# Seven block products instead of eight in the gate and up projections of one FFN

## The chip, the cores and the metric

The kernel runs on one core of a Trainium2 chip. The metric is the time of one execution on the device, in microseconds (us). The times of the kernel before were 2115.74, 2116.9 and 2116.8 us, median 2116.8.

## The reference

Two transformer blocks over 512 tokens of width 1024, in float32. The change touches one piece of the first block, its second feed-forward layer:

```
u = modulate(rmsnorm(h, norm3_g), shift, scale)
h = h + 0.5 * gate * ((silu(u @ w_g) * (u @ w_u)) @ w_down)
```

`w_g` and `w_u` are the two halves of `ffn2_w_gu`, each 1024 x 2816; `w_down` is 2816 x 1024. The feature dimension 2816 is 22 tiles of 128.

## The kernel before, in words

Activations lie with features on the 128 partitions and the 512 tokens along the row, so `h` is eight tiles of 128x512. Every float32 operand of a large product is cut into a rounded part `hi` (type float32r) and the rest `lo`, and a product is three matmuls: hi x hi, hi x lo and lo x hi. For weights `split_w` does this: ScalarE rounds a 128x1024 piece (L131), VectorE subtracts (L132). Split weights live in two rings of four buffers (`whi`, `wlo`), raw weights in a ring of two (`raw`), loaded by SP's queue.

`proj` (L155 to L164) forms one 128x512 result in a PSUM bank: for each of the eight k tiles three matmuls of 512 columns. `ffn_first` runs the layer. For each feature tile f it loads the gate and the up columns, splits them, calls `proj` twice, takes Silu on ScalarE (L482), multiplies on VectorE (L484) and splits the result (L485, L486) into `m_hi`, `m_lo`. After 8, 16 and 22 tiles a down projection adds that part to `h` (L497): eight output tiles j, with 8, 8 and 6 k tiles; in the last part the tiles j = 6 and 7 go in two halves of 256 columns. In the second layer (`halved=True`) the first feature tile is also worked in two halves of tokens, because `u` becomes available half by half: `Modulated` gathers the row statistics while `h` is being finished, and `modulate` makes `hi` and `lo` of `u` from them (L304, L307, L308).

The order of instructions on each engine is made by a planner that walks the program in order and takes, at each step of its own timeline, the first instruction that is ready; waits are semaphores between the engines. POOL, whose queue issues the DMAs that the hardware generators can't do, has no work in this stage.

Of the kernel before, what the change touches and what calls it, by code (L numbers as in the profile page):

```python
# [25 lines left out]
def kernel(  # L26
# [7 lines left out]
    nc = tc.nc  # L34
# [6 lines left out]
    sp = ctx.enter_context(tc.tile_pool(name="sp", bufs=2))  # L41
# [40 lines left out]
    with tc.tile_pool(name="stage", bufs=1) as stage:  # L82
# [16 lines left out]
        def raw_tile():  # L99
            return wp.tile([P, 8 * 256], F32, tag="raw", name="w_raw")  # L100
# [23 lines left out]
        def split_w(src, hi=None, lo=None):  # L124
            if hi is None:
                shape = [P, src.shape[1], src.shape[2]]
                hi, lo = (
                    wp.tile([P, 8 * P], F32R, tag=tag, name=tag, bufs=4)[
                        :, 0:shape[1] * shape[2]].rearrange("p (k n) -> p k n", n=shape[2])
                    for tag in ("whi", "wlo"))  # L130
            nc.scalar.activation(out=hi, in_=src, func=AF.Copy)  # L131
            nc.vector.tensor_tensor(out=lo, in0=src, in1=hi.bitcast(F32), op=ALU.subtract)  # L132
            return hi, lo

        def by_feature(raw, kt=KT):
            v = raw[:, 0:kt * 256].rearrange("p (k n) -> p k n", n=256)
            return [split_w(v[:, :, r * P:(r + 1) * P]) for r in range(2)]
# [17 lines left out]
        def proj(acc, w, u, k0=0, cols=slice(0, S)):  # L155
            whi, wlo = w
            n = len(u)
            for k in range(n):
                uhi, ulo = u[k]
                a = whi[:, k0 + k, :]  # L160
                b = wlo[:, k0 + k, :]
                nc.tensor.matmul(acc, lhsT=a, rhs=uhi[:, cols], start=k == 0, stop=False)  # L162
                nc.tensor.matmul(acc, lhsT=a, rhs=ulo[:, cols], start=False, stop=False)  # L163
                nc.tensor.matmul(acc, lhsT=b, rhs=uhi[:, cols], start=False, stop=k == n - 1)  # L164
# [13 lines left out]
        def split_act(src, pool, tag, bufs=None):  # L178
            kw = {} if bufs is None else {"bufs": bufs}
            hi = pool.tile([P, S], F32R, tag=tag + "h", name=tag + "_hi", **kw)  # L180
            lo = pool.tile([P, S], F32R, tag=tag + "l", name=tag + "_lo", **kw)
            nc.scalar.activation(out=hi, in_=src, func=AF.Copy)
            nc.vector.tensor_tensor(out=lo, in0=src, in1=hi.bitcast(F32), op=ALU.subtract)
            return hi, lo
# [51 lines left out]
        def shift(sub, j):  # L236
            f = (sub * 3) * KT + j
            return modc[:, f:f + 1]

        def gmod(sub, j):  # L240
            return gmod_t[:, sub, j:j + 1]

        def gate(sub, j):
            return gate_t[:, sub, j:j + 1]


        h = [hp.tile([P, S], F32, name=f"h{j}") for j in range(KT)]
# [23 lines left out]
        class Stat:  # L271
            def __init__(self):
                self.acc = sp.tile([P, S], F32, tag="acc", name="acc", bufs=2)

            def add(self, j, cols=ALL, scale=1.0):
                if j == 0:
                    nc.scalar.activation(out=self.acc[:, cols], in_=h[j][:, cols], func=AF.Square,
                                         scale=scale)
                    return
                sq = sp.tile([P, S], F32, tag="wk", name="sq")  # L280
                nc.scalar.activation(out=sq[:, cols], in_=h[j][:, cols], func=AF.Square,
                                     scale=scale)
                nc.vector.tensor_add(out=self.acc[:, cols], in0=self.acc[:, cols],
                                     in1=sq[:, cols])
# [11 lines left out]
        def new_u():  # L296
            return [tuple(up.tile([P, S], F32R, tag=tag, name=tag) for tag in ("uh", "ul"))
                    for _ in range(KT)]
# [19 lines left out]
        class Modulated:  # L318
# [13 lines left out]
            def operand(self):  # L332
                u = new_u()
                for pb, cols in self.pieces:
                    modulate(self.sub, u, pb, cols)
                return u

        def down_tiles(src, kt, by_halves=True):

            pieces = {}  # L340
            steps = [(j, ALL) for j in range(KT)]
            if by_halves:
                steps = steps[:6] + [(j, cols) for cols in HALVES for j in range(6, KT)]
            for j, cols in steps:
                q = j // 2
                if q not in pieces:
                    pieces[q] = by_feature(load_w(src[:, 256 * q:256 * (q + 1)], kt, 256), kt)
                yield j, cols, pieces[q][j % 2]
# [110 lines left out]
    parts = ((0, 8), (8, 16), (16, 22))  # L459


    def ffn_first(u, w_gu, w_down, sub, on_final, nxt=None, side=None, early=(), halved=False):
        with tc.tile_pool(name=f"ffn{sub}", bufs=2) as fp:
            for pi, (f0, f1) in enumerate(parts):
                ms = []
                for f in range(f0, f1):
                    if f < len(early):
                        raw = early[f]
                    else:
                        raw = load_pair(w_gu[:, f * P:(f + 1) * P],  # L470
                                        w_gu[:, FF + f * P:FF + (f + 1) * P], KT, P)
                    wg, wu = by_feature(raw)
                    hi = fp.tile([P, S], F32R, tag="mh", name="m_hi", bufs=14)
                    lo = fp.tile([P, S], F32R, tag="ml", name="m_lo", bufs=14)
                    for cols in HALVES if halved and f == 0 else (ALL,):
                        n = cols.stop - cols.start
                        pg = mm_bank()[:, 0:n]
                        proj(pg, wg, u, cols=cols)
                        pu = mm_bank()[:, 0:n]
                        proj(pu, wu, u, cols=cols)  # L480
                        sg = fp.tile([P, S], F32, tag="sg", name="sg")[:, 0:n]
                        nc.scalar.activation(out=sg, in_=pg, func=AF.Silu)  # L482
                        m = fp.tile([P, S], F32, tag="m", name="m")[:, 0:n]
                        nc.vector.tensor_mul(out=m, in0=sg, in1=pu)  # L484
                        nc.scalar.activation(out=hi[:, cols], in_=m, func=AF.Copy)  # L485
                        nc.vector.tensor_tensor(out=lo[:, cols], in0=m,  # L486
                                                in1=hi[:, cols].bitcast(F32), op=ALU.subtract)
                    ms.append((hi, lo))
                    if side is not None:
                        side(f, fp)  # L490
                kt = f1 - f0
                last = pi == len(parts) - 1
                for j, cols, w in down_tiles(w_down[f0 * P:f1 * P], kt, last):
                    pd = mm_bank()[:, 0:cols.stop - cols.start]
                    with behind(nxt, j, cols):
                        proj(pd, w, ms, cols=cols)
                    nc.vector.scalar_tensor_tensor(out=h[j][:, cols], in0=pd,  # L497
                                                   scalar=gate(sub, j), in1=h[j][:, cols],
                                                   op0=ALU.mult, op1=ALU.add)
                    if last:  # L500
                        on_final(j, cols)
# [17 lines left out]
    with ExitStack() as mx:  # L519
# [140 lines left out]
        with tc.tile_pool(name="mrg", bufs=2) as gp:  # L660
# [28 lines left out]
            for j, cols, w in down_tiles(w_out[0], KT):  # L689
# [3 lines left out]
                nc.vector.scalar_tensor_tensor(out=h[j][:, cols], in0=pd, scalar=gate(1, j),  # L693
                                               in1=h[j][:, cols], op0=ALU.mult, op1=ALU.add)
                nxt.add(j, cols)
    u = nxt.operand()


    wi = w_in_2[0]
# [21 lines left out]
            u2[j] = tuple(up.tile([P, S], F32R, tag=tag, name=tag) for tag in ("uh", "ul"))  # L721
        scaled(j, gcomb, u2[j], cols)

    ffn_first(u, ffn2_w_gu[0], ffn2_w_down[0], 2, end_of_first, halved=True)
    u = u2

    def bcast_sb(inv, pool):
# [517 lines left out]
```

## Time and profile before

| what | value |
|---|---|
| median of 3 runs | 2116.8 us |
| the profiled execution | 2115.97 us |
| its span | 2114.3 us |
| granted TensorE clock, mean | 0.996 of 2.4 GHz |
| TensorE, VectorE, ScalarE, POOL busy | 99%, 55%, 39%, 4% |

The span is measured inside the execution; 1.7 us lie around it. A matmul's busy time overlaps with the next one's, so the cost of a matmul is read from the distance of two starts. The changed layer stands at about 781 to 1147 us of the span.

### The profile page before, as it was taken

Reading aid. Unit: us, or ns where it says so; the run is one execution under the profiler, and the core shown is the slowest. Engines: PE = TensorE matmul, PEld = TensorE weight load, DVE = VectorE, ACT = ScalarE, POOL = GpSimd, SP = SyncE. Lnnn points to the kernel's source line nnn. Section 1 sums busy time; section 2 is a strip of 40 time slices with the busy share of each in tenths; the row PEclk is TensorE's granted clock in tenths of the full one; section 3 lists DMA queues with packets and bytes.
Section 4 is the critical chain, followed back from the end, with each engine's and each line's share of the span. In section 5 each row is a group of like instructions: output and inputs, shape, how many; then the busy total and the mean of one; then the engine's idle time right before and its main releaser. Section 6 shows DMA issues by size and latency. Waiting matters only on the chain.

```text
span 2114.3 us, 24896 instructions
## 1 busy us (share of the span) xinstructions
PE 2086.4 (99%) x9814; PEld 1698.0 (80%) x9814; DVE 1163.6 (55%) x1988; ACT 824.4 (39%) x1284; POOL 94.1 (4%) x156
## 2 busy tenths in 40 slices
PE   7999999999999999999999999999999999999998
PEld 5778888888878888888888876767888888888888
DVE  3775645466653454333336486746454566474675
ACT  4322222357653333222225354645233344242454
POOL 1000000000000000000000011112200000000000
PEclk9999999999999999999999999999999999999999
DMA  9776654331122333333322332213323333333332
GB/s 347 217 226 179 179 179 119 101 99 61 60 81 81 101 99 82 98 100 100 100 85 95 97 94 80 80 50 100 120 80 100 100 85 96 100 100 100 90 106 94
DMA packets 302216, 235.72 MB, mean 111 GB/s; under 512 B 6821, under 2 KB 289130, under 8 KB 301844
## 3 DMA queue, kind: packets, MB, share of 16 engines
q1 hardware_dynamic: 298752, 223.96, 35.2%
q0 software_dynamic: 2656, 9.09, 1.3%
q8 instruction: 77, 1.26, 0.3%
q10 hardware_dynamic: 692, 1.09, 0.1%
q14 instruction: 39, 0.32, 0.0%
HBM read 229.89 MB, written 4.23 MB: 111 GB/s over the span
## 4 chain that ended last, share of the span: by engine, by line
PE 97%; ACT 1%; DVE 1%; DMA 1%; issue 0%; POOL 0%; POOLq 0%; SPq 0%; ACTq 0%; DVEq 0%
PE mm_ps L162 27%; PE mm_ps L163 27%; PE mm_ps L164 27%; PE mm_ps L174 2%; PE mm_ps L175 2%; PE mm_ps L176 2%; PE po_ps L929 2%; PE z_ps L604 1%; PE z_ps L922 1%; PE z_ps L883 1%; PE po_ps L615 1%; PE z_ps L885 1%; DMA wa<-in_w_ada_dram 0%; PE z_ps L207 0%; PE z_ps L1044 0%
## 5 line engine op out<-in xcount | busy, mean ns | idle before, releaser
L131 ACT ACTIVATE whi<-w_raw 128x1024 fp32r<-128x1024 f32 (+1 forms) x350 | 365.0, 1045 | 892.2 <-PE mm_ps L163 694.1
L162 PE MATMUL mm_ps<-uh,whi 128*128 128x512 f32 (+1 forms) x1680 | 653.3, 391 | 3.8 <-ACT uh L307 3.3
L163 PE MATMUL mm_ps<-ul,whi 128*128 128x512 f32 (+1 forms) x1680 | 653.9, 390 | 0.0
L164 PE MATMUL mm_ps<-uh,wlo 128*128 128x512 f32 (+1 forms) x1680 | 653.2, 389 | 0.0
L132 DVE TENSOR_TENSOR wlo<-w_raw,whi 128x1024 fp32r<-128x1024 f32 (+1 forms) x350 | 426.6, 1221 | 233.6 <-ACT whi L131 227.9
L162 PEld LDWEIGHTS mm_ps<-uh,whi 128*128 128x128 f32 x1680 | 316.1, 189 | 71.4 <-ACT uh L307 4.7
L164 PEld LDWEIGHTS mm_ps<-uh,wlo 128*128 128x128 f32 x1680 | 316.8, 189 | 64.9 <-issue 1.6
L163 PEld LDWEIGHTS mm_ps<-ul,whi 128*128 128x128 f32 x1680 | 316.8, 189 | 63.5 <-issue 0.8
L164 PE MATMUL mm_ps<-m_hi,wlo 128*128 128x512 f32 (+1 forms) x564 | 212.1, 376 | 0.0
L162 PE MATMUL mm_ps<-m_hi,whi 128*128 128x512 f32 (+1 forms) x564 | 211.7, 377 | 0.0
L163 PE MATMUL mm_ps<-m_lo,whi 128*128 128x512 f32 (+1 forms) x564 | 211.6, 375 | 0.0
L163 PEld LDWEIGHTS mm_ps<-m_lo,whi 128*128 128x128 f32 x564 | 106.1, 188 | 20.1 <-issue 0.4
L164 PEld LDWEIGHTS mm_ps<-m_hi,wlo 128*128 128x128 f32 x564 | 106.1, 188 | 19.9
L162 PEld LDWEIGHTS mm_ps<-m_hi,whi 128*128 128x128 f32 x564 | 106.0, 188 | 19.8 <-issue 0.8
L174 PE MATMUL mm_ps<-whi,uh 128*128 128x512 f32 (+1 forms) x288 | 99.9, 350 | 3.6 <-ACT whi L131 1.6
L175 PE MATMUL mm_ps<-wlo,uh 128*128 128x512 f32 (+1 forms) x288 | 98.7, 344 | 0.8 <-DVE wlo L132 0.8
L176 PE MATMUL mm_ps<-whi,ul 128*128 128x512 f32 (+1 forms) x288 | 97.4, 343 | 0.0
L497 DVE SCALAR_TENSOR_TENSOR h<-mm_ps,gate,h 128x512 f32<-128x512 f32 (+1 forms) x52 | 36.9, 709 | 100.5 <-PE mm_ps L164 100.3
L484 DVE TENSOR_TENSOR m<-sg,mm_ps 128x512 f32<-128x512 f32 (+1 forms) x45 | 30.4, 675 | 107.8 <-PE mm_ps L164 107.2
L200 DVE SCALAR_TENSOR_TENSOR ada_acc<-ada_w,csil,ada_acc 128x256 f32<-128x256 f32 x196 | 87.4, 482 | 1.9
L1118 DVE SCALAR_TENSOR_TENSOR y<-xp,cols_c,y 128x512 f32<-128x512 f32 x88 | 65.7, 749 | 2.3 <-ACT y L1114 0.7
L174 PEld LDWEIGHTS mm_ps<-whi,uh 128*128 128x128 f32 x288 | 54.4, 189 | 11.3 <-ACT uh L307 2.0
(314 smaller groups left out, 2304.0 us busy)
## 6 DMA issues: line engine op xcount, KB each, us to landing
w_raw<-in_ffn_w_gu_dram SPq DMA_DIRECT2D x88, 512.0 KB, 5.2
ada_w<-in_w_ada_dram SPq DMA_DIRECT2D x28, 1024.0 KB, 5.2
w_raw<-in_w_up_dram SPq DMA_DIRECT2D x44, 512.0 KB, 5.2
w_raw<-in_w_in_dram SPq DMA_DIRECT2D x20, 1024.0 KB, 5.2
w_raw<-in_ffn_w_down_dram SPq DMA_DIRECT2D x16, 1024.0 KB, 5.1
w_raw<-in_w_mix_in_dram SPq DMA_DIRECT2D x24, 512.0 KB, 5.3
wa<-in_w_ada_dram SPq DMA_DIRECT2D x8, 1024.0 KB, 11.2
w_raw<-in_w_mix_in_dram SPq DMA_DIRECT2D x8, 1024.0 KB, 5.0
```

The lines of the kernel that those rows point to most:

```text
L131: nc.scalar.activation(out=hi, in_=src, func=AF.Copy)
L132: nc.vector.tensor_tensor(out=lo, in0=src, in1=hi.bitcast(F32), op=ALU.subtract)
L162: nc.tensor.matmul(acc, lhsT=a, rhs=uhi[:, cols], start=k == 0, stop=False)
L163: nc.tensor.matmul(acc, lhsT=a, rhs=ulo[:, cols], start=False, stop=False)
L164: nc.tensor.matmul(acc, lhsT=b, rhs=uhi[:, cols], start=False, stop=k == n - 1)
L174: nc.tensor.matmul(acc, lhsT=a, rhs=wh, start=k == 0, stop=False)
L175: nc.tensor.matmul(acc, lhsT=a, rhs=wl, start=False, stop=False)
L176: nc.tensor.matmul(acc, lhsT=b, rhs=wh, start=False, stop=k == kt - 1)
L200: nc.vector.scalar_tensor_tensor(out=acc[:, q, :], in0=v[:, k, :], scalar=csil[:, k:k + 1], in1=acc[:, q, :], op0=ALU.mult, op1=ALU.add)
L497: nc.vector.scalar_tensor_tensor(out=h[j][:, cols], in0=pd, scalar=gate(sub, j), in1=h[j][:, cols], op0=ALU.mult, op1=ALU.add)
L929: nc.tensor.matmul(po[64 * hd:64 * hd + 64, b * P:S], lhsT=vts[head // 4][:, b, c0:c0 + 64], rhs=pT, start=b == 0, stop=b == NB - 1, skip_ ...
L1118: nc.vector.scalar_tensor_tensor(out=y, in0=xp[:, k:k + S], scalar=cols_c[:, 44 * k + col:44 * k + col + 1], in1=y, op0=ALU.mult, op1=ALU.add)
```

## The change

In `ffn_seven` twenty of the 22 feature tiles are worked in pairs. The product of a pair's weights with `u` is taken as a 2 x 2 block product: upper and lower block row are the 256 gate and the 256 up columns, the inner dimension is cut into its two halves of 512, the tokens into two halves of 256. Strassen's scheme (in Winograd's form) forms it with seven block products instead of eight. Each block product (`times`) is two row tiles x four k tiles x three matmuls of 256 columns.

- **Sums of `u`** (`operand`): made once, for each of four k, four VectorE operations of 128x256, one rounding of 128x1024 on ScalarE and one subtraction on VectorE. They need `u` unsplit, so `modulate_full` writes it with one more ScalarE instruction per tile and half. The sums stand in the ring `ra` of four buffers, before the blocks `w11` and `w21` of the weights use it.
- **Sums of weights**: four DMAs per pair, issued by POOL, SBUF to SBUF with `accum_op=add`, 128x1024 floats each. Splits in order: `w11`, `w12`, then after adds `w11`, `w21`, `w11`, `w11`, and `w22`: seven of 128x1024 per pair instead of four.
- **Recombining**: three ScalarE copies out of PSUM and five VectorE sums or differences of 128x512 per pair.
- The first two tiles stay as they were, the first in halves. The down projections come after 6, 12, 18 and 22 tiles, each one pair of gate and up products later than its data.

```diff
+            p1 = split_w(w11)
+            add(w11, w21)
+            ca = z_bank()
+            self.times(ca, p1, self.plain(0, H1), True)
+            v1 = copy(ca)
+            p2 = split_w(w12)
+            self.times(ca, p2, self.plain(HK, H1), False)
+            upper(ca, 0)
+            q7 = split_w(w11)
+            add(w21, w22)
+            add(w11, w22)
+            cd = z_bank()
+            self.times(cd, q7, self.diff(2), True)
+            v7 = copy(cd)
+            q5 = split_w(w21)
+            cc = z_bank()
+            self.times(cc, q5, self.diff(0), True)
+            v5 = copy(cc)
+            q6 = split_w(w11)
+            add(w11, w12)
+            cb = z_bank()
+            self.times(cb, q6, self.diff(1), True)
+            nc.vector.tensor_add(out=v1, in0=v1, in1=cb)
+            nc.vector.tensor_add(out=v5, in0=v5, in1=v1)
+            nc.vector.tensor_sub(out=v7, in0=v7, in1=v5)
+            q3 = split_w(w11)
+            self.times(cc, q3, self.plain(HK, H2), False)
+            nc.vector.tensor_add(out=v5, in0=cc, in1=v1)
+            upper(v5, 1)
+            lower(v7, 1)
+            q4 = split_w(w22)
+            self.times(cd, q4, self.diff(3), False)
+            nc.vector.tensor_sub(out=v1, in0=cd, in1=v1)
+            lower(v1, 0)
...
+        def operand(self, u, full):
+            self.u = u
+            for k in range(HK):
+                t = self.pool.tile([P, 4, 256], F32, tag="ra", name="usum", bufs=4)
...
+                nc.vector.tensor_sub(out=t[:, 0], in0=b11, in1=b12)
+                nc.vector.tensor_sub(out=t[:, 2], in0=b12, in1=b22)
+                nc.vector.tensor_sub(out=t[:, 1], in0=t[:, 2], in1=b11)
+                nc.vector.tensor_add(out=t[:, 3], in0=t[:, 1], in1=b21)
...
+            def add(to, of):
+                nc.gpsimd.dma_start(out=to, in_=of, accum_op=ALU.add)
...
+            nc.scalar.activation(out=hi, in_=t, func=AF.Identity, bias=shift(sub, j))
+            nc.scalar.activation(out=full[j][:, cols], in_=t, func=AF.Identity,
+                                 bias=shift(sub, j))
+            nc.vector.tensor_tensor(out=lo, in0=full[j][:, cols], in1=hi.bitcast(F32),
+                                    op=ALU.subtract)
...
+            bounds = ((0, 6), (6, 12), (12, 18), (18, 22))
+            pairs = [eight_pair(0)]
+            seven.operand(u, full)
+            for f0, f1 in bounds:
+                last = f1 == NF
+                for f in range(f0 + 2, min(f1 + 2, NF), 2):
+                    pairs.append(seven_pair(f))
...
-    ffn_first(u, ffn2_w_gu[0], ffn2_w_down[0], 2, end_of_first, halved=True)
+    ffn_seven(nxt, ffn2_w_gu[0], ffn2_w_down[0], 2, end_of_first)
```

## Rows read from the trace of the kernel before

**Rows 1.** The page's busy table and the chain that ended last.
```profile
PE 2086.4 (99%) x9814; PEld 1698.0 (80%) x9814; DVE 1163.6 (55%) x1988; ACT 824.4 (39%) x1284; POOL 94.1 (4%) x156
...
PE 97%; ACT 1%; DVE 1%; DMA 1%; issue 0%; POOL 0%; POOLq 0%; SPq 0%; ACTq 0%; DVEq 0%
```

**Rows 2.** Windows: stretch, busy of each engine, granted clock, DMA share, GB/s.
```profile
800.00:930.00 130.00, 129.86 (x578) 107.41 (x578) 47.10 (x51) 35.86 (x44) 0.00 (x0) 1.00 0.34 97
```

**Rows 3.** Waits, 790 to 1160 us: who waited for whom, total, times, longest.
```profile
ACT whi L131 <- PE mm_ps L163: 180.8, 48, 6.1
DVE wlo L132 <- ACT whi L131: 82.2, 44, 4.9
```

**Rows 4.** Timeline of ScalarE: start, duration, instruction; Silus of whole tiles.
```profile
815.43 0.58 ACT L482 ACTIVATE sg<-mm_ps 128x512 f32<-128x512 f32 x1
...
869.83 0.58 ACT L482 ACTIVATE sg<-mm_ps 128x512 f32<-128x512 f32 x1
```

**Rows 5.** Timeline of TensorE, last down projection, matmuls of 256 columns.
```profile
1143.39 0.28 PE L164 MATMUL mm_ps<-m_hi,wlo 128*128 128x256 f32 x1
...
1146.63 0.28 PE L164 MATMUL mm_ps<-m_hi,wlo 128*128 128x256 f32 x1
```

**Rows 6.** Lines by form, 790 to 1160 and 781 to 810 us: busy, mean ns.
```profile
L131 ACT ACTIVATE whi<-w_raw 128x1024 fp32r<-128x1024 f32 x60 | 63.6, 1061 | 218.9 <-PE mm_ps L163 158.3 <-issue 60.6
L132 DVE TENSOR_TENSOR wlo<-w_raw,whi 128x1024 fp32r<-128x1024 f32 x60 | 73.5, 1227 | 76.6 <-ACT whi L131 75.0
L497 DVE SCALAR_TENSOR_TENSOR h<-mm_ps,gate,h 128x512 f32<-128x512 f32 x22 | 16.5, 751 | 57.4 <-PE mm_ps L164 57.3
L484 DVE TENSOR_TENSOR m<-sg,mm_ps 128x512 f32<-128x512 f32 x21 | 14.4, 688 | 70.4 <-PE mm_ps L164 70.4
L486 DVE TENSOR_TENSOR m_lo<-m,m_hi 128x512 fp32r<-128x512 f32 x21 | 14.4, 685 | 0.0
L485 ACT ACTIVATE m_hi<-m 128x512 fp32r<-128x512 f32 x21 | 13.3, 631 | 0.2
L482 ACT ACTIVATE sg<-mm_ps 128x512 f32<-128x512 f32 x21 | 12.2, 582 | 0.0
L283 DVE TENSOR_TENSOR acc<-acc,sq 128x256 f32<-128x256 f32 x8 | 3.1, 418 | 0.0
...
L307 ACT ACTIVATE uh<-ut,modc 128x256 fp32r<-128x256 f32 x16 | 7.6, 504 | 6.6 <-DVE ut L304 6.6
```

**Rows 7.** DMA issues: transfer, queue, times, KB each, median us to landing.
```profile
w_raw<-in_ffn_w_gu_dram SPq DMA_DIRECT2D x88, 512.0 KB, 5.2
...
cb<-cum_d POOLq DMA_DIRECT2D x16, 256.0 KB, 3.5
...
w_raw<-in_w_ple_gate_dram SPq DMA_DIRECT2D x4, 1024.0 KB, 8.4
...
pl<-ple_d POOLq DMA_DIRECT2D x1, 2048.0 KB, 8.3
...
wsr<-in_gmlp_w_s_dram POOLq DMA_DIRECT2D x1, 512.0 KB, 4.3
...
gfb<-in_norm_final_g_dram POOLq DMA_DIRECT2D x1, 512.0 KB, 10.6
```

**Rows 8.** Lines of POOL: the issue of a DMA.
```profile
L871 POOL DMA_DIRECT2D cb<-cum_d x16 | 9.0, 563 | 122.3 <-DVE low L893 54.1 <-issue 39.6 <-DVE off L889 23.4
```

**Rows 9.** Windows at the stage's start, columns as in rows 2.
```profile
781.00:790.00 9.00, 7.43 (x46) 7.16 (x47) 8.27 (x20) 4.46 (x11) 0.70 (x1) 0.81 0.44 117
790.00:800.00 10.00, 9.67 (x65) 8.76 (x64) 7.53 (x18) 5.64 (x11) 0.00 (x0) 1.00 0.01 2
```

**Rows 10.** Timeline of VectorE at the stage's start; in brackets the idle time before.
```profile
797.76 0.49 DVE L308 SCALAR_TENSOR_TENSOR ul<-ut,modc,uh 128x256 fp32r<-128x256 f32 x1 [0.18 <-ACT uh L307]
803.13 1.22 DVE L132 TENSOR_TENSOR wlo<-w_raw,whi 128x1024 fp32r<-128x1024 f32 x1 [4.89 <-ACT whi L131]
```

More of the change, by code (lines that the diff above doesn't have):

```diff
@@ L459, with ffn_first @@
     parts = ((0, 8), (8, 16), (16, 22))
-    def ffn_first(u, w_gu, w_down, sub, on_final, nxt=None, side=None, early=(), halved=False):
+    def ffn_first(u, w_gu, w_down, sub, on_final, nxt=None, side=None, early=()):
         with tc.tile_pool(name=f"ffn{sub}", bufs=2) as fp:
@@ L472, in ffn_first @@
                     wg, wu = by_feature(raw)
[L473 to L488, printed above, removed]
+                    pg = mm_bank()
+                    proj(pg, wg, u)
+                    pu = mm_bank()
+                    proj(pu, wu, u)
+                    sg = fp.tile([P, S], F32, tag="sg", name="sg")
+                    nc.scalar.activation(out=sg, in_=pg, func=AF.Silu)
+                    m = fp.tile([P, S], F32, tag="m", name="m")
+                    nc.vector.tensor_mul(out=m, in0=sg, in1=pu)
+                    ms.append(split_act(m, fp, "m", 14))
                     if side is not None:
@@ new lines, in modulate_full @@
+    def modulate_full(sub, u, full, pb, cols):
+        for j in range(KT):
+            hi, lo = (t[:, cols] for t in u[j])
+            t = sp.tile([P, S], F32, tag="wk", name="ut")[:, cols]
+            nc.vector.scalar_tensor_tensor(out=t, in0=h[j][:, cols], scalar=gmod(sub, j),
+                                           in1=pb[:, 0:cols.stop - cols.start],
+                                           op0=ALU.mult, op1=ALU.mult)
+            nc.scalar.activation(out=hi, in_=t, func=AF.Identity, bias=shift(sub, j))
[3 more added lines that the diff above has]
+                                    op=ALU.subtract)
@@ new lines, in ffn_seven, with split_m, m_pair, eight_pair @@
+    def ffn_seven(nxt, w_gu, w_down, sub, on_final):
+        with tc.tile_pool(name=f"ffn{sub}", bufs=4) as fp:
+            u = new_u()
+            full = []
+            for _ in range(HK):
+                t = fp.tile([P, 2, S], F32, tag="mh", name="u_full")
+                full += [t[:, 0], t[:, 1]]
+            for pb, cols in nxt.pieces:
+                modulate_full(sub, u, full, pb, cols)
+            seven = Seven(fp)
+            def split_m(m, hi, lo):
+                nc.scalar.activation(out=hi, in_=m, func=AF.Copy)
+                nc.vector.tensor_tensor(out=lo, in0=m, in1=hi.bitcast(F32), op=ALU.subtract)
+            def m_pair():
+                return tuple(fp.tile([P, 2, S], F32R, tag=tag, name=name)
+                             for tag, name in (("mh", "m_hi"), ("ml", "m_lo")))
+            def eight_pair(f0):
+                pair = m_pair()
+                for r in range(2):
+                    f = f0 + r
+                    wg, wu = by_feature(load_pair(w_gu[:, f * P:(f + 1) * P],
+                                                  w_gu[:, FF + f * P:FF + (f + 1) * P], KT, P))
+                    for cols in (ALL,) if r else HALVES:
+                        n = cols.stop - cols.start
+                        pg = mm_bank()[:, 0:n]
+                        proj(pg, wg, u, cols=cols)
+                        pu = mm_bank()[:, 0:n]
+                        proj(pu, wu, u, cols=cols)
+                        sg = seven.ev()[:, 0:n]
+                        nc.scalar.activation(out=sg, in_=pg, func=AF.Silu)
+                        nc.vector.tensor_mul(out=sg, in0=sg, in1=pu)
+                        split_m(sg, *(t[:, r, cols] for t in pair))
+                return pair
+            def seven_pair(f0):
+                pair = m_pair()
+                cols = slice(f0 * P, (f0 + 2) * P)
+                weights = seven.load(w_gu[:, cols], w_gu[:, FF + f0 * P:FF + (f0 + 2) * P])
+                sg = {}
+                def upper(src, half):
+                    sg[half] = src if half else seven.ev()
+                    nc.scalar.activation(out=sg[half], in_=src, func=AF.Silu)
+                def lower(src, half):
+                    nc.vector.tensor_mul(out=src, in0=src, in1=sg[half])
+                    split_m(src.rearrange("p (r s) -> p r s", r=2),
+                            *(t[:, :, HALVES[half]] for t in pair))
+                seven.run(weights, upper, lower)
+                return pair
+            bounds = ((0, 6), (6, 12), (12, 18), (18, 22))
[5 more added lines that the diff above has]
+                    pairs.append(seven_pair(f))
+                kt = f1 - f0
+                ms = [tuple(t[:, r, :] for t in pair) for pair in pairs[:kt // 2]
+                      for r in range(2)]
+                del pairs[:kt // 2]
+                for j, cols, w in down_tiles(w_down[f0 * P:f1 * P], kt, last):
+                    pd = mm_bank()[:, 0:cols.stop - cols.start]
+                    proj(pd, w, ms, cols=cols)
@@ L695 @@
                 nxt.add(j, cols)
-    u = nxt.operand()
     wi = w_in_2[0]
```

63 lines of the change are left out of this document (added).

## The prediction

> **What bounds the kernel now.** I read the page's busy table and its chain of waits first, then the stage, then the spacing of matmuls, then the engines beside them. TensorE is busy 99% of the span and holds 97% of the chain that ended last [rows 1]: time goes only where matmuls go, or where TensorE is made to wait. The changed stage runs from about 781 us (first modulated operand) to 1147 us (last down projection). Inside it TensorE is busy 129.86 of 130 us while VectorE has 47.10 and ScalarE 35.86, at a granted clock of 1.00, the upper level, 2.4 GHz [rows 2]. The split of a weight tile (ScalarE L131, VectorE L132) waits longest for a matmul that frees its buffer [rows 3]: weights are ahead of TensorE. So the stage is a dense stream of matmuls with spare room on VectorE, ScalarE and the DMA engines (share 0.34).
>
> **Matmuls removed.** Successive Silus of whole tiles stand 10.88 us apart (815.43 to 869.83 us, five steps) [rows 4]; a tile has 48 matmuls of 512 columns, so one costs 226.7 ns. The matmuls of 256 columns in the last down projection start at 1143.39 and, 27 later, 1146.63 us [rows 5]: 120.0 ns. Half the columns cost 0.53 of the time, about 13 ns fixed each. A pair of tiles was 96 x 0.2267 = 21.76 us. Seven products of 2 rows x 4 k x 3 matmuls are 168 x 0.120 = 20.16 us, not 7/8 of 21.76 (19.04). Gain 1.60 us a pair, 16.0 us for ten pairs. The last down part shrinks from 6 to 4 k tiles, so 72 matmuls in halves become 48: 24 fewer, each 120.0 - 113.4 ns too dear, 0.2 us. Other down matmuls are only regrouped. TensorE gain: 16.2 us.
>
> The Trainium skill (TensorE: Matmul & The Clock Gate, Back-to-back issue gap) has a gap of columns / 2.4 GHz plus 2.5 ns, 215.8 and 109.2 ns here; by it a pair would save 20.72 - 18.35 = 2.37 us, the sum 23.7 us. The trace has 226.7 and 120.0 ns, so I keep 16.0.
>
> **VectorE and ScalarE.** Per pair now: seven splits of 128x1024, 1.061 us on ScalarE and 1.227 us on VectorE each, instead of four; five recombining operations of 128x512 at 0.688 us, two products at 0.688, two subtractions at 0.685; on ScalarE three copies at about 0.6, two Silus at 0.582, two roundings at 0.631 [rows 6]. VectorE 8.6 + 3.4 + 1.4 + 1.4 = 14.8 us, ScalarE 7.4 + 1.8 + 1.2 + 1.3 = 11.7 us, in 20.16 us of matmuls. Neither is the bound by itself. Eight more updates of h, 0.751 us each, lie beside the down matmuls. Without that cover the added VectorE work, 7 us a pair, would be 70 us.
>
> **The adding DMAs.** Four a pair, 512 KB each, on POOL's queue, whose issue takes 0.56 us [rows 8] and delays nothing (POOL has no other work here). They are in a chain: split p1, add, split q7, add, split q6, add, split q3. No row shows a DMA that adds, nor one from SBUF to SBUF. On that queue 256 KB land in 3.5 us, 512 KB in 4.3, 2048 KB in 8.3 [rows 7]. An add reads source and destination and writes one. Lower bound 3.5 us, upper 8.3. Nearest are 4.3 (bytes counted once) and 4.3 + 512/1536 x 4.0 = 5.6 (twice); I take L = 5.0.
>
> Does L fit? A product lasts 24 x 0.120 = 2.88 us. Four buffers for split weights let a split start when the product four earlier ends, three products before its own. With p1 starting at 0, q7's split may start at -2.88, q3 is due at 14.4. Between lie three splits (1.061 + 1.227 = 2.29 each) and two adds: q3 is ready at -2.88 + 6.87 + 2L, late by 2L - 10.4 us. At L = 5.0 that is 0.4 us of slack; it runs out at 5.2. One evacuation of 0.69 us ahead of the split on VectorE uses up the 0.4 and leaves 0.3; six pairs do not follow a down projection: 1.8 us. The three that do have 1.2 us more, as down products (18 x 0.2267 = 4.08 us) free buffers earlier relative to them. Bounds: 0 at 3.5; at 8.3, 6 x 6.2 + 3 x 5.0 = 52 us.
>
> **The start.** Modulation is a ping-pong of ut, uh, ul. The copy `full` adds 16 x 0.504 = 8.1 us to ScalarE [rows 6], which between 781 and 800 us is busy 4.46 + 5.64 of 19 [rows 9]: it fits, but nearly fills it, and ul now waits behind it. Taken: 1.5 us (0 if it falls into the idle pieces, 8.1 if all of it lengthens the ping-pong). Then the operand sums: 16 x 0.418 + 4 x 1.227 = 11.6 us of VectorE, which today idles 4.89 us from 798.25 to 803.13 us [rows 10]. The sums use the four "ra" buffers that w11 and w21 of the first pair need. Step by step: sums 0 and 1 from 799.5 us, lo 0 done at 804.1, lo 1 with a weight split between about 807; w11 lands 5.2 us later [rows 7] at 809.3, w21 at 812.2. p1 is split at 811.6. TensorE would be done with the first two tiles at 815.43 - 5.44 = 810.0 (24 matmuls before the Silu of the third): waits 1.6. p2 ends at 817.4; add 1 lands at 817.2, q7 is split at 819.5: 2.1. Add 2 lands at 822.2, q5 is split at 824.5 against 822.4: 2.1. q6 is ready at 826.8, in time (827.4). Add 4 lands at 831.8, q3 is split at 834.1 against 830.3: 3.8. Into this last wait the next pair's p1 and p2 can be ordered, which need no new sum; I count it as filled. Cost 1.5 + 1.6 + 2.1 + 2.1 = 7.3 us; 11.1 with nothing filled, 0 if sums and loads were hidden, 21 at the upper L. The clock may add to it: over 781 to 790 us, where TensorE waits now, the grant was 0.81 [rows 9]; once more of that would be 9 x 0.19 = 1.7 us, which I leave to the range.
>
> **The end.** The last pair is consumed at once. After its last matmul come a subtraction, a product and a rounding (0.69 + 0.69 + 0.63 us and hand-overs, 2.4 together); the two k tiles of the pair before give 6 x 0.2267 = 1.4 us of cover: 1.0 us (0 if another j's first matmuls are put there, 1.7 with the lo part). Today seven k tiles cover it.
>
> **Sum.** -16.2 + 7.3 + 1.8 + 1.0 = -6.1 us against the profiled execution, 2115.97 us (span 2114.3, 1.7 around it): 2109.9. The median shown, 2116.8, lies 0.8 above it, so on its scale 2110.7.
>
> **Rivals.** Differences within 0.2%, 4.2 us, cannot be told from none, so faster means below 2112.6, slower above 2121.0.
>
> *The adds are too slow (slower).* Place: q3 of each pair, and q7 of the first. With nothing filled in, the sum passes zero at L of about 5.4 and +4.2 us at about 5.7. At L = 6: 6 x 1.6 + 3 x 0.4 = 10.8 us late, start 1.5 + 1.6 + 3.1 + 3.1 + 4.8 = 14.1, end 1.0, less 16.2: +9.7, 2126.5. At L = 7: 28.8 + 17.1 + 1.0 - 16.2 = +30.7, 2147.5. For it: an add moves more than a plain copy of its size, and adds travel beside weight loads. When a 2048 KB and a 512 KB transfer ran on POOL's queue near the end, the 512 KB took 10.6 us and the weight loads beside them 8.4 instead of 5.2 [rows 7]. Against: the stage's DMA share is 0.34, and TensorE's order can put p1 and p2 of the next pair, 5.8 us, ahead of a late q3. Chance 0.28.
>
> The Trainium skill (DMA: Bandwidth & Descriptors, Issuing engines are not separate DMA queues) says that DMAs from all issuing engines run on the same 16 engines and interleave. The trace's 8.4 and 10.6 us agree.
>
> *The gain is spent at the start.* Nothing fills the wait for q3 (11.1 us) and VectorE's order costs each of ten pairs one 0.3 us: -16.2 + 11.1 + 3.0 + 1.0 = -1.1, 2115.7. For it: a 73% busy in-order VectorE. Against: it has whole stretches under the down matmuls. Chance 0.22.
>
> *The start is hidden.* Sums go into VectorE's 4.89 us gap and the loads land in time, only q7 waits 2.1: 2103.7. Against: buffers tie the loads to the sums. Chance 0.10.
>
> Forecast 0.40, own range 2107 to 2114.
>
> **Numbers.** Faster: 0.36 of the forecast and the hidden start, 0.46. Same: 0.04 of it, 0.16 of the spent gain, 0.01 of the slow adds, 0.21. Slower: 0.27 and 0.06, 0.33. The range leaves out half of the hidden start and the worst of the slow adds (L above about 6.6): 2103 to 2140.
>
> **What would show it.** Right: matmuls of 256 columns 120 ns apart and 20.2 us between pairs in the middle of the stage; adds landing in about 5 us; TensorE idle 5 to 9 us around 800 to 835 us and hardly after. Wrong: adds over 5.6 us with TensorE waiting on VectorE L132 in each pair; 256-column matmuls dearer than 120 ns; or a granted clock below 1 after the waits.

## The result and the profile after

The changed kernel takes 2170.3 us (median of 4 runs, 2168.69 to 2173.78), the kernel before 2116.27 us beside it: ratio 1.0258, 95% interval 1.024 to 1.0275. It is slower by 54 us, where the forecast was 6 us faster and the range ended at 2140. The profiled execution took 2169.28 us, its span is 2167.5 us, 53.2 us more than before. All times are medians; one run each of vector_adds and last_by_vector below, at a mean granted clock of 0.65, took about 2950 us and is left out of theirs.

The page of the changed kernel, busy table and chain of waits (they answer to [rows 1]):

```profile
PE 2099.1 (97%) x10522; PEld 1737.5 (80%) x10522; DVE 1242.4 (57%) x2104; ACT 882.7 (41%) x1372; POOL 127.7 (6%) x196
...
PE 47%; ACT 1%; issue 1%; DVE 1%; DMA 0%; POOL 0%; POOLq 0%; ACTq 0%; DVEq 0%
```

TensorE is no longer busy all the time, and its share of the chain that ended last falls from 97% to 47%: the shares listed make up half of the span, and the rest has no line of its own there, so the page only says that matmuls are no longer all of the path. VectorE and ScalarE hardly moved, so neither has become the bound by its load. The stage tells more. Windows of the changed kernel, columns as in [rows 2]:

```profile
800.00:850.00 50.00, 41.27 (x269) 38.01 (x268) 27.81 (x37) 21.17 (x28) 6.23 (x7) 0.91 0.62 150
850.00:900.00 50.00, 42.15 (x302) 40.45 (x302) 23.88 (x28) 19.26 (x25) 4.35 (x5) 0.92 0.61 150
900.00:950.00 50.00, 50.00 (x299) 44.74 (x298) 26.29 (x31) 16.63 (x21) 4.36 (x5) 1.00 0.53 137
950.00:1000.00 50.00, 41.60 (x299) 39.98 (x298) 23.58 (x28) 20.56 (x27) 6.09 (x7) 0.90 0.61 138
1000.00:1050.00 50.00, 49.77 (x274) 44.08 (x274) 25.09 (x30) 13.62 (x17) 3.48 (x4) 0.97 0.57 151
1050.00:1100.00 50.00, 43.16 (x322) 41.72 (x321) 26.93 (x31) 21.14 (x28) 6.10 (x7) 0.93 0.62 145
1100.00:1150.00 50.00, 47.05 (x247) 40.67 (x247) 25.24 (x30) 15.71 (x20) 3.48 (x4) 0.97 0.43 112
```

TensorE idles 8.7 + 7.9 + 0 + 8.4 + 0.2 + 6.8 + 3.0 = 35 us, and the granted clock falls short of 1.00 by 0.09 + 0.08 + 0 + 0.10 + 0.03 + 0.07 + 0.03, times 50 us: by that estimate 20 us more. The fullest stretches hold a down projection. How one leads to the other, windows of 2 us in the second pair:

```profile
844.00:846.00 2.00, 0.00 (x0) 0.00 (x0) 0.00 (x0) 1.00 (x2) 0.82 (x1) 1.00 0.01 2
...
848.00:850.00 2.00, 2.00 (x12) 2.00 (x11) 0.00 (x0) 0.17 (x1) 0.47 (x1) 0.50 0.93 172
...
852.00:854.00 2.00, 2.00 (x19) 2.00 (x18) 0.51 (x2) 1.12 (x2) 0.00 (x0) 1.00 0.28 74
```

TensorE stands still at 844 to 846 us; at 848 to 850 us the grant is 0.50, the level of 1.2 GHz, and 12 matmuls fall into the window, against 19 at 2.4 GHz (852 to 854 us). So a part of the waits is paid a second time. Who waits for whom, 781 to 1210 us ([rows 3] of before; `z_ps` is the PSUM bank of a block product, L536 its first matmul of three; `uth` and `utl` below are the parts of the sums of `u`):

```profile
ACT whi L131 <- DMA w_sum<-w_raw: 69.5, 28, 5.7
...
ACT whi L131 <- DMA w_sum<-w_sum: 30.4, 7, 8.3
PE z_ps L536 <- ACT whi L131: 29.1, 19, 3.0
```

Before, the splits waited for TensorE; now ScalarE's split waits for the adds (99.9 us), and TensorE for the split (29.1 us in 19 stops). The adds themselves, DMA issues of the same stretch ([rows 7]):

```profile
w_sum<-w_raw POOLq DMA_DIRECT2D x30, 512.0 KB, 4.6
...
w_sum<-w_sum POOLq DMA_DIRECT2D x10, 512.0 KB, 6.7
```

The median is 4.6 us for the second to fourth add of a pair, 6.7 us for the first. One period, from the second pair's first add to the third pair's. POOL's issues of adds 1 to 4 and of the next add 1, start and, in brackets, the idle time before:

```profile
835.29 0.87 POOL L578 DMA_DIRECT2D w_sum<-w_sum  x1 [8.62 <-DVE wlo L132]
845.17 0.87 POOL L578 DMA_DIRECT2D w_sum<-w_raw  x1 [9.01 <-DMA w_sum<-w_sum]
847.60 0.87 POOL L578 DMA_DIRECT2D w_sum<-w_raw  x1 [1.56 <-DVE wlo L132]
855.15 0.87 POOL L578 DMA_DIRECT2D w_sum<-w_raw  x1 [6.68 <-DVE wlo L132]
865.74 0.87 POOL L578 DMA_DIRECT2D w_sum<-w_sum  x1 [9.71 <-DVE wlo L132]
```

and ScalarE's splits in the same stretch (and of its other instructions the copies of p1's product, 845.96, and of q5's, 856.76):

```profile
845.00 1.06 ACT L131 ACTIVATE whi<-w_sum 128x1024 fp32r<-128x1024 f32 x1 [2.22 <-DMA w_sum<-w_sum]
845.96 0.58 ACT L582 ACTIVATE ev<-z_ps 128x512 f32<-128x512 f32 x1
...
849.83 1.06 ACT L131 ACTIVATE whi<-w_sum 128x1024 fp32r<-128x1024 f32 x1 [3.29 <-DMA w_sum<-w_raw]
...
852.54 1.06 ACT L131 ACTIVATE whi<-w_sum 128x1024 fp32r<-128x1024 f32 x1 [0.69 <-DMA w_sum<-w_raw]
...
856.76 0.60 ACT L582 ACTIVATE ev<-z_ps 128x512 f32<-128x512 f32 x1 [2.22 <-PE z_ps L543]
860.25 1.06 ACT L131 ACTIVATE whi<-w_sum 128x1024 fp32r<-128x1024 f32 x1 [2.90 <-DMA w_sum<-w_raw]
861.22 1.04 ACT L131 ACTIVATE whi<-w_raw 128x1024 fp32r<-128x1024 f32 x1
862.16 1.04 ACT L131 ACTIVATE whi<-w_sum 128x1024 fp32r<-128x1024 f32 x1
```

Read together they are one chain. From the issue of add 1 to the start of q7's split, which needs it, pass 9.71 us; to q5's split, which needs add 2, 4.83 more; to q6's, which needs add 3, 2.71; to the issue of add 4 2.61; to q3's split, which needs it, 5.10. Behind q3's split stand q4's, the third pair's p1 (862.16) and p2, and the next add 1 goes out 5.49 after q3's split began. Sum 30.45 us, where TensorE needs 20.16. This period is the longest: the six of the stage that hold no down projection last 24.5 to 30.5 us. The third pair's p1 needs no sum at all. Its weights' load was issued at 832.75 us, and the buffer that it takes, the fourth before it, is that of q5, whose product is done when it is copied out at 856.76. It is split at 862.16, because it stands behind q3 and q4 on ScalarE, which works in order.

Not only splits stand behind a waiting split. TensorE's stop in this period is

```profile
846.10 0.39 PE L536 MATMUL z_ps<-uth,whi 128*128 128x256 f32 x1 [2.81 <-ACT whi L131]
```

on q7's first matmul. p2's product, 2.88 us of work, could have filled it, for p2 had been split since 836.1 us. But on TensorE it stands behind q7's first two matmuls, and it needs the bank of p1's product copied out, which ScalarE does at 845.96, behind q7's split. What another order there would give was not tried.

### The profile page after: what moved, and what is told of

Same layout as the page of the kernel before. It is cut to its first block, busy times and chain, and to the rows that moved or that the text cites. A ratio compares the mean times of both kernels' runs of the same rounds, so it can differ in the third digit from the quotient of the medians.

```text
span 2167.5 us, 26690 instructions
## 1 busy us (share of the span) xinstructions
PE 2099.1 (97%) x10522; PEld 1737.5 (80%) x10522; DVE 1242.4 (57%) x2104; ACT 882.7 (41%) x1372; POOL 127.7 (6%) x196
## 4 chain that ended last, share of the span: by engine, by line
PE 47%; ACT 1%; issue 1%; DVE 1%; DMA 0%; POOL 0%; POOLq 0%; ACTq 0%; DVEq 0%
PE mm_ps L162 12%; PE mm_ps L164 12%; PE mm_ps L163 12%; PE mm_ps L174 2%; PE mm_ps L175 2%; PE mm_ps L176 2%; PE po_ps L1133 2%; PE z_ps L1126 1%; PE z_ps L1087 1%; PE z_ps L1089 1%; PE z_ps L543 0%; PE z_ps L541 0%; PE z_ps L536 0%; PE z_ps L1248 0%; DMA w_sum<-w_raw 0%
## 5 line engine op out<-in xcount | busy, mean ns | idle before, releaser
L131 ACT ACTIVATE whi<-w_raw 128x1024 fp32r<-128x1024 f32 (+2 forms) x338 | 344.4, 1023 | 704.7 <-PE mm_ps L163 550.4
L162 PE MATMUL mm_ps<-uh,whi 128*128 128x512 f32 (+1 forms) x1360 | 529.4, 391 | 5.1 <-ACT uh L307 2.0
L163 PE MATMUL mm_ps<-ul,whi 128*128 128x512 f32 x1360 | 529.5, 390 | 0.0
L164 PE MATMUL mm_ps<-uh,wlo 128*128 128x512 f32 x1360 | 528.4, 389 | 0.0
L132 DVE TENSOR_TENSOR wlo<-w_raw,whi 128x1024 fp32r<-128x1024 f32 (+2 forms) x338 | 402.3, 1193 | 149.7 <-ACT whi L131 145.6
L162 PEld LDWEIGHTS mm_ps<-uh,whi 128*128 128x128 f32 x1360 | 255.8, 189 | 60.7 <-ACT uh L307 3.9
L164 PEld LDWEIGHTS mm_ps<-uh,wlo 128*128 128x128 f32 x1360 | 256.0, 188 | 52.1 <-issue 1.6
L162 PE MATMUL mm_ps<-m_hi,whi 128*128 128x512 f32 (+1 forms) x560 | 211.6, 381 | 0.9 <-ACT whi L131 0.5
L162 PEld LDWEIGHTS mm_ps<-m_hi,whi 128*128 128x128 f32 x560 | 105.4, 188 | 21.1 <-ACT whi L131 0.9
L132 DVE TENSOR_TENSOR wlo<-w_sum,whi 128x1024 fp32r<-128x1024 f32 x50 | 61.2, 1225 | 103.8 <-ACT whi L131 103.0
L536 PE MATMUL z_ps<-uth,whi 128*128 128x256 f32 x320 | 94.6, 296 | 18.7 <-ACT whi L131 18.6
L174 PE MATMUL mm_ps<-whi,uh 128*128 128x512 f32 (+1 forms) x288 | 100.7, 353 | 5.9 <-ACT zv L1190 2.9
L131 ACT ACTIVATE whi<-w_sum 128x1024 fp32r<-128x1024 f32 x50 | 52.9, 1058 | 126.4 <-DMA w_sum<-w_raw 69.5
L543 PE MATMUL z_ps<-uth,wlo 128*128 128x256 f32 x320 | 93.7, 293 | 3.6 <-DVE wlo L132 3.6
L541 PE MATMUL z_ps<-utl,whi 128*128 128x256 f32 x320 | 92.8, 290 | 0.0
```

The costliest lines, as they stand in the source:

```text
L174: nc.tensor.matmul(acc, lhsT=a, rhs=wh, start=k == 0, stop=False)
L536: i = nc.tensor.matmul(a, lhsT=whi[:, k, rows], rhs=uhi, start=start and first is None, stop=False, skip_group_check=True)
L541: nc.tensor.matmul(a, lhsT=whi[:, k, rows], rhs=ulo, start=False, stop=False, skip_group_check=True)
L543: nc.tensor.matmul(a, lhsT=wlo[:, k, rows], rhs=uhi, start=False, stop=last, skip_group_check=True)
```

## The experiments

Theory 1: the order of the splits ties the adds of one pair and the first add of the next into one serial chain, which is longer than TensorE's work. Rivals: the adds' traffic slows TensorE, the loads or the buffers (theory 2); or the scheme itself (more splits, recombining, regrouped down projections) costs the time (theory 3). All were timed in three rounds beside the kernel before; the intervals are 95%.

**no_adds**: everything but the adds, so the sums of weights are not formed and the result is not the layer's.

```diff
-                nc.gpsimd.dma_start(out=to, in_=of, accum_op=ALU.add)
+                pass
```

> Leaves out the four adding DMAs of each pair, so the block products are of the blocks as loaded (their sums are not formed); everything else stays. Theory 1 (the chain: a pair lasts as long as add, split, add, split, add, split in a row, because ScalarE splits the next pair's p1 only behind q3, which waits for the last add): the chain is gone, the pair is bound by its 168 matmuls of 120 ns, 20.2 us; the stage keeps -16.2 us and pays about 5 us at its start and end: 2104 to 2112. Theory 2 (transfers: the adding DMAs are late because they share the engines with weight loads, whatever the order): the same 2104 to 2112. Theory 3 (no gain to be had: short matmuls, VectorE and ScalarE work eat it): above 2125 with TensorE still waiting for splits.

Measured 2105.57 us, ratio 0.9952 (0.9937 to 0.9967); the span is 2103.5 us. Its first window of 50 us:

```profile
800.00:850.00 50.00, 50.00 (x388) 48.44 (x387) 36.41 (x47) 28.23 (x37) 0.00 (x0) 1.00 0.39 122
```

TensorE is full at 1.00, and so it is in the five windows up to 1100 us. So the adds cost 65 us, and the scheme without them is 10 us faster than the kernel before. Splits and recombining are hidden. Theories 1 and 2 expect this alike; theory 3 is out.

**vector_adds**: the same sums, made by VectorE.

```diff
-                nc.gpsimd.dma_start(out=to, in_=of, accum_op=ALU.add)
+                nc.vector.tensor_add(out=to, in0=to, in1=of)
```

> The same sums by VectorE (four tensor_add of 128x1024, about 1.23 us each) instead of DMAs; the result is complete. Theory 1: each add step shrinks from 5 to 9 us to about 1.5, the chain of a pair to 3 x (1.5 + 2.3) + 5 = 16 us, under 20.2; VectorE has 14.8 + 4.9 = 19.7 us a pair and is nearly the bound: 2106 to 2118. Theory 2: no added transfers: 2106 to 2118 as well. Theory 3: VectorE becomes the bound, above 2130.

Measured 2108.38 us, ratio 0.9962 (0.995 to 0.9975): faster than both kernels. Lines by form of this kernel, busy and mean ns:

```profile
L578 DVE TENSOR_TENSOR w_sum<-w_sum,w_raw 128x1024 f32<-128x1024 f32 x30 | 36.6, 1219 | 0.3
```

A sum takes 1.22 us instead of a landing of 4.6 to 9.7. VectorE had the room (43.49 of 50 us in the first window, 32 to 40 later), and TensorE waited for a `whi` 0.6 us in all.

**pool_adds**: the same sums on POOL (`nc.gpsimd.tensor_add` in the same line).

> The same sums by POOL's tensor_add of 128x1024 (2.8 to 2.9 us each in the trace of before) instead of DMAs; the result is complete. Theory 1: chain 3 x (2.9 + 2.5) + 5 = 21 us a pair, just over 20.2: 2108 to 2124. Theory 2: no added transfers, so like the run without adds, 2104 to 2112. Theory 3: above 2125.

Measured 2126.81 us, ratio 1.0051 (1.0036 to 1.0066). Lines by form:

```profile
L578 POOL TENSOR_TENSOR w_sum<-w_sum,w_raw 128x1024 f32<-128x1024 f32 x30 | 79.2, 2640 | 74.2 <-DVE wlo L132 73.4
...
L132 DVE TENSOR_TENSOR wlo<-w_raw,whi 128x1024 fp32r<-128x1024 f32 x33 | 55.3, 1676 | 12.6 <-ACT whi L131 11.8
```

A sum takes 2.64 us here, between the other two, and the time lies between theirs. But it is 2.8 us above theory 1's range, in theory 3's, and far above theory 2's, though no transfer is added. VectorE's subtraction of the raw weights takes 1.68 us on average instead of 1.22: ten subtractions take 2.3 to 3.4 us, each beside a sum of POOL, and those beside none take 1.22. One of them, and POOL's sum beside it:

```profile
908.25 3.19 DVE L132 TENSOR_TENSOR wlo<-w_raw,whi 128x1024 fp32r<-128x1024 f32 x1
```

```profile
907.96 2.40 POOL L578 TENSOR_TENSOR w_sum<-w_sum,w_raw 128x1024 f32<-128x1024 f32 x1
```

TensorE's waits for `whi` at L536 fall to 2.7 us, and its largest wait in the stage is for that subtraction:

```profile
PE z_ps L543 <- DVE wlo L132: 8.0, 5, 3.5
```

So this run is no clean test of the length of a sum; what the slower subtraction adds was not tried by itself.

**hoist**: the next pair's loads, the split of its p1 and its first add stand ahead of q3's split, within a run of pairs. The adds stay DMAs. Six of the nine distances between pairs are changed so; three hold a down projection.

```diff
             self.times(cb, q6, self.diff(1), True)
...
+            ahead()
             q3 = split_w(w11)
...
+        def begin(self, a1, a2):
+            weights = self.load(a1, a2)
+            p1 = split_w(weights[0])
+            self.add(weights[0], weights[2])
+            return weights, p1
```

> The adding DMAs stay as they are, but in a run of pairs the next pair's load, split of p1 and first add stand in the program before the split of q3 of the pair at work (seven places; not across a down projection). Theory 1: the next pair's first add, 7 to 10 us, then runs beside the wait for the last add instead of behind it; 5 to 8 us saved at each of six or seven places, partly eaten because p1 takes one of four split buffers early: 2125 to 2150. Theory 2: the transfers stay, so no change: 2165 to 2175. Theory 3: no change.

Measured 2134.54 us, ratio 1.0088 (1.0071 to 1.0105): 36 us of the 65 are gone by order alone, with the same forty DMAs. (The loads move too, and the median landing of a first add goes from 6.7 to 5.3 us.) In the trace the next pair's first add now follows add 4 directly, and lands beside it:

```profile
924.19 0.87 POOL L572 DMA_DIRECT2D w_sum<-w_raw  x1 [7.00 <-DVE wlo L132]
926.25 0.87 POOL L572 DMA_DIRECT2D w_sum<-w_sum  x1 [1.19 <-DVE wlo L132]
```

2.06 us apart instead of 10.59 (855.15 to 865.74) in the changed kernel. From first add to first add it is 16.3 to 23.1 us within a run of pairs, instead of 24.5 to 30.5. TensorE's waits for `whi` at L536 fall from 29.1 to 13.2 us.

**own_buffers**: as hoist, and the halves of p1 get a buffer of their own (the recombining ring shrinks from 6 to 4 for it), in case the ring of split weights is what is short.

```diff
+            p1 = split_w(weights[0], *(self.pool.tile([P, HK, 256], F32R, tag=tag, name=tag, bufs=1)
+                                       for tag in ("p1h", "p1l")))
...
-            return self.pool.tile([P, S], F32, tag="ev", name="ev", bufs=6)
+            return self.pool.tile([P, S], F32, tag="ev", name="ev", bufs=4)
```

> Like the run with the next pair's load, split of p1 and first add ahead of q3's split, and p1's halves get a buffer of their own instead of one of the four (the recombining buffers go from 6 to 4 for the room). Theory 1: q7's split is then held neither by p1's buffer nor by q3's place on ScalarE, so it can start some 11 us before its use; two adds of 5 us and three splits of 2.3 us after it fit into 14.4 + 11 us; nothing waits within a run of pairs, the first pair and the pairs behind a down projection wait as in the run before: 2112 to 2126. Theory 2: the transfers stay, so no better than that run, 2130 or more.

Measured 2134.03 us, ratio 1.0088 (1.0071 to 1.0104), as hoist. The expectation failed. The waits for `whi` fall to 3.7 us, but another stands in their place:

```profile
PE z_ps L536 <- ACT ev L691: 8.3, 2, 7.2
...
PE z_ps L536 <- ACT whi L131: 3.7, 5, 1.2
```

Two stops wait for a Silu (L691) that frees its PSUM bank and writes into the recombining ring, which the edit itself had shortened. The longer stop, 7.2 us, ends behind the Silu of 859.82 us. ScalarE has no idle time before that Silu: it stands behind three splits, of which the first had waited for an add,

```profile
856.97 1.06 ACT L131 ACTIVATE whi<-w_sum 128x1024 fp32r<-128x1024 f32 x1 [8.31 <-DMA w_sum<-w_raw]
```

so a split that needs a sum holds up this instruction as well. Whether the shorter ring gave the Silu its late place was not tried apart, so this run doesn't say what the ring of split weights costs.

**adds_aside**: each add reads its operand and goes into one tile that nobody reads, so the sums of weights are not formed.

```diff
+            self.side = pool.tile([P, HK, 256], F32, name="side", bufs=1)
+            nc.gpsimd.memset(self.side, 0.0)
...
-                nc.gpsimd.dma_start(out=to, in_=of, accum_op=ALU.add)
+                nc.gpsimd.dma_start(out=self.side, in_=of, accum_op=ALU.add)
```

> The four DMAs of a pair are issued at the same places, with the same sources and sizes, but add into a tile of their own that nothing reads, so the sums of weights are not formed: the added traffic stays, the splits no longer wait for it. Theory 1 (only the wait in the chain costs): like the run without adds, 2104 to 2112. Theory 2 (the transfers themselves are in the way, by delaying the weight loads): 2120 to 2150.

Measured 2125.43 us, ratio 1.0045 (1.003 to 1.006), 20 us above no_adds: in theory 2's range, not in theory 1's. Windows and waits:

```profile
850.00:900.00 50.00, 35.65 (x220) 32.61 (x219) 17.71 (x23) 12.86 (x19) 6.10 (x7) 0.83 0.64 143
...
1000.00:1050.00 50.00, 50.00 (x358) 47.31 (x357) 27.67 (x30) 21.24 (x27) 6.96 (x8) 1.00 0.79 179
```

```profile
POOL side L580 <- DMA side<-w_raw: 146.2, 29, 8.9
...
ACT whi L131 <- DMA w_raw<-in_ffn_w_down_dram: 32.0, 3, 24.9
...
PE mm_ps L162 <- ACT whi L131: 11.5, 1, 11.5
```

With a DMA share of 0.79, above any of the changed kernel's windows, TensorE is full at 1.00: the traffic does not slow matmuls. The loss lies in one window: a stop of 11.5 us at the first down projection, one of 2.9 us before it, and the low clock. Adds into one tile follow one another, each waiting for the last to land, and so hold the raw buffers that the down projection's load needs: that load is issued at 889.48 us. So a load is late here, as theory 2 says, but for a buffer and not for the traffic, and by the experiment's own chain of adds. In the changed kernel the matmuls of down projections wait for a `whi` 0.5 us in all (L162 of its page).

**all_eight**: all tiles by eight products in the changed kernel's frame (regrouped down projections, `full`, the sums of `u`).

```diff
-                    pairs.append(seven_pair(f))
+                    pairs.append(eight_pair(f))
```

> All 22 tiles by the eight-product way; what stays of the change is the unsplit copy of u, the sums of u (made and not used) and the down projections after 6, 12, 18 and 22 tiles. Both theories: the cost of these parts alone, the sums beside the first tiles: 2116 to 2122. If it were 2130 or more, a part of the loss would be neither chain nor transfers.

Measured 2123.24 us, ratio 1.0032 (1.002 to 1.0044), 1 us above the expected range: the frame alone costs 7 us. Where, is read from the start of the value projection, the first work after the stage. TensorE at L174, first to last start, of before, then no_adds (in all_eight it starts at 1147.6, in the changed kernel at 1193.1, in vector_adds at 1134.0):

```profile
L174 PE MATMUL mm_ps<-whi,uh x64: 389/389/496, 1146.8 to 1198.4; 128*128 128x512 f32 x64
```

```profile
L174 PE MATMUL mm_ps<-whi,uh x64: 389/389/507, 1132.8 to 1185.6; 128*128 128x512 f32 x64
```

all_eight loses 0.8 us up to there and 4.0 of its 4.8 us of span behind it; no_adds gains 14.0 and gives 3.2 back. The stretch that gives it back lies far behind the stage, in code that wasn't edited. In vector_adds it shows in this window, which before has TensorE at 95.95 us and a clock of 1.00:

```profile
1400.00:1500.00 100.00, 94.83 (x409) 72.80 (x409) 52.65 (x95) 37.25 (x65) 28.42 (x16) 0.97 0.27 86
```

1.1 us of idle time and 3 us of clock. TensorE waits there for ScalarE (`zv`, L1190) 2.6 us instead of 0.7; all_eight and the changed kernel show the same wait (2.6 and 2.9). That the planner ordered the later work otherwise may be the cause; it was not tried by itself.

**last_by_vector** and **two_by_vector**: theory 1 by parts. The fourth sum, or the third and the fourth, are made by VectorE; the others stay DMAs.

```diff
-            add(w11, w12)
+            nc.vector.tensor_add(out=w11, in0=w11, in1=w12)
```

and in the second also

```diff
-            add(w11, w22)
+            nc.vector.tensor_add(out=w11, in0=w11, in1=w22)
```

> Only the fourth sum of each pair (the one that q3 needs) is made by VectorE instead of an adding DMA; the other three stay adding DMAs. Theory 1 (the order of the splits makes the adds of a pair and the first add of the next pair one serial chain): the chain of a pair gets shorter by the landing of one add less a VectorE sum, 4.9 - 1.2 = 3.7 us, in each of the nine distances between pairs, which were 24.5 to 30.4 us; that is 33 us, and the clock gives back a few more: 2125 to 2137 us. Rival (each adding DMA costs TensorE its own share of time, wherever it stands): a quarter of the 65 us that the four adds cost goes, about 2154 us. Rival (the q3 add alone is late, as forecast): all but the start's cost goes, 2108 to 2114 us.

> The third and fourth sum of each pair (those of q6 and q3) are made by VectorE, the first and second stay adding DMAs. Theory 1: only one landing (7 to 9.7 us) is left in the chain of a pair, with splits and two sums of 1.2 us about 20 us, close to what TensorE needs (20.16 us): 2106 to 2116 us. Rival (each adding DMA costs its own share): half of the 65 us stays, about 2138 us.

Measured 2137.57 us, ratio 1.0091 (1.0074 to 1.0107), and 2127.9 us, 1.0048 (1.0031 to 1.0065), beside 2118.03 us of before. The first is 0.6 us above theory 1's range and far from both rivals: one add of four brings half of the 65 us back, so the adds don't cost equal shares. Nor is a late q3 alone the cause, or all but the start's waits would be gone. The second missed by 12 us, because the expectation overlooked a landing: q6's split stands behind q5's on ScalarE, and q5 still waits for add 2. Its POOL issues and its first two splits with sums:

```profile
831.14 0.87 POOL L578 DMA_DIRECT2D w_sum<-w_sum  x1 [14.24 <-DVE wlo L132]
...
854.55 0.87 POOL L578 DMA_DIRECT2D w_sum<-w_sum  x1 [14.03 <-DVE wlo L132]
```

```profile
839.47 1.06 ACT L131 ACTIVATE whi<-w_sum 128x1024 fp32r<-128x1024 f32 x1 [4.82 <-DMA w_sum<-w_sum]
...
844.29 2.01 ACT L131 ACTIVATE whi<-w_sum 128x1024 fp32r<-128x1024 f32 x2 [2.24 <-DMA w_sum<-w_raw]
```

The period is 23.41 us (831.14 to 854.55): 8.33 us to q7's split, 4.82 to q5's, and 10.26 of splits, two VectorE sums and the next p1. It is the same serial chain with two landings in it, and still longer than 20.16.

## Why the prediction was wrong

**The step that failed** is "Four buffers for split weights let a split start when the product four earlier ends, three products before its own." It takes buffers for the only thing that holds a split back. ScalarE works in order, and in its order each split that needs a sum holds up all splits behind it, those that need none too. At 862.16 us the next pair's p1 is split 1.91 us behind q3's split, for which add 4 had to land; its first add goes out only then. So the two adds that the forecast put between q7's and q3's splits (2L - 10.4 us late) are not a chain that starts afresh in each pair at -2.88 us: its start is itself late by the lateness of the pair before. The period is the whole loop, 24.5 to 30.5 us in the trace, not 20.16 and 0.3. The size of L is not what failed: with the forecast's 5.0 us in place of the 9.71 the loop shown above would still be 25.7 us (an estimate). hoist removes this link within the runs of pairs and brings back 36 of the 65 us.

How much: the split of p1 of the first and of the tenth pair, in the changed kernel

```profile
807.80 1.06 ACT L131 ACTIVATE whi<-w_sum 128x1024 fp32r<-128x1024 f32 x1 [1.38 <-DMA w_sum<-in_ffn_w_gu_dram]
...
1137.60 1.06 ACT L131 ACTIVATE whi<-w_sum 128x1024 fp32r<-128x1024 f32 x1 [3.23 <-PE mm_ps L163]
```

stand 329.8 us apart; in vector_adds they start at 807.35 and 1078.50, 271.2 apart. These nine distances hold 58.6 of the 59.1 us by which the value projection starts later than there (1193.1 against 1134.0), between 2.0 and 9.0 us each, 23.5 of them in the three that hold a down projection. The forecast had 1.8 us for all of them, and the waits of the start, which lie in the first.

**The clock** was left to the range as 1.7 us at the start. The windows have 20 us: as the waits came back, so did the lower level. "A granted clock below 1 after the waits" stood among what would make the prediction wrong, but with no price.

**L** was right for three of four adds, 4.6 us against 5.0. The first add of a pair was mis-sized: 6.7 us in the middle and 9.71 us to the split in the period above. The six that go out in the same microseconds as the next weight loads (DMA share 0.84 at 834 to 836 us) land in 6.6 to 9.6 us, the four others in 4.5 to 5.0. And the forecast left this add out of its chain: by its own rule p1's split can start at -8.64 us, so that add 1 lands at -8.64 + 2.29 + 5.0 = -1.35, behind the -2.88 that it took for q7. The rival with slow adds had the right sign but the wrong reason: at the measured L its own formula gives no loss, and even at L = 7 it ends at 2147.5. It looked for TensorE waiting on VectorE L132; that is 3.6 us in the stage, the wait on ScalarE L131 29.1. Its 8.4 us for weight loads is the middle of 5.1 us for a load ahead of the two transfers and 11.6 us for one beside them.

**Matmuls** came out as forecast. In the changed kernel

```profile
930.51 0.28 PE L536 MATMUL z_ps<-uh,whi 128*128 128x256 f32 x1
...
933.98 0.28 PE L543 MATMUL z_ps<-uth,wlo 128*128 128x256 f32 x1
```

29 steps take 3.47 us, 119.7 ns each; and no_adds, which has neither waits nor adds, reaches the value projection 14.0 us earlier, against -16.2 + 1.5 + 1.6 + 1.0 = -12.1 of the forecast without adds. The 1.6 us for the first pair's loads don't show: TensorE has no idle time from 800 to 835 us. For modulation it idles 1.7 us more than before from 781 to 800 us, but at a grant of 1.00 instead of 0.91, which gives as much back. The end was not measured by itself. **VectorE and ScalarE** are not the bound, as said; vector_adds even loads VectorE with the sums.

**The start** was right in its steps: add 1 goes out at 810.82 us (forecast: p1 split at 811.6), q7 is split from 815.51, q5 from 820.35, q3 from 830.41. With the 2.29 us of a split the first ends at 817.8, the others at 822.6 and 832.7, 1.4 to 1.9 us earlier than forecast. TensorE idles 5.9 us from 800 to 834 us, by the windows; the forecast's three waits there were 5.8. That the sums agree is luck: 3.2 us of the 5.9 lie from 828 to 834 us, in the wait for q3, which the forecast counts as filled (at 830 to 832 us TensorE has 0.48 of 2 us), and the other waits were shorter.

**Left out** altogether: 3 to 7 us that the kernels with pairs lose behind the stage (no_adds and the changed kernel).

**Open**: hoist still stands 29 us above no_adds. Its windows from 800 to 1150 us have 17 us of idle time, of which 13.2 us are waits for `whi` and some belong to the start, which hoist doesn't touch; two windows at a clock of 0.97 are 3 us more, and 4 us lie behind the stage. The rest was not taken apart, nor what the ring of split weights costs alone.

## What to carry to other kernels

When data come by a long detour into an engine that works in order, follow the whole loop to the same instruction of the next round: what stands behind the waiting instruction, and whether the next round's first step is among it. If the loop is longer than the bound engine's round, its excess is paid in every round. Here a latency of 5 us was dearer than 1.2 us of work on an engine that had room; and a short repeated stop of TensorE should be priced with the clock that falls behind it.

## What the runs showed of the hardware

- An adding DMA of 512 KB from SBUF to SBUF lands in 4.6 us (median of 30). Of the ten first adds of a pair the six beside weight loads land in 6.6 to 9.6 us, the four with few or none beside them in 4.5 to 5.0. Its issue on POOL takes 0.87 us, against 0.56 for the plain one of [rows 8], which moves 256 KB.
- The sum of 128x1024 floats takes 1.22 us on VectorE and 2.64 us on average on POOL (2.40 at the least). Ten of VectorE's subtractions of that size in pool_adds take 2.3 to 3.4 us, each beside a sum of POOL; one beside none takes 1.22.
- With the DMA share at 0.79 the matmuls kept their pace: in adds_aside 29 steps of 256 columns from 1015.56 us take 3.47 us too.
- In the changed kernel TensorE stood still for 2.81 us up to 846.10 us; the grant was 0.50 at 848 to 850 us with TensorE busy, and 1.00 from 852 us on.
